# Three pairs of projection units computed with seven block products instead of eight

## The chip, the cores and the metric

The kernel runs on one NeuronCore of a Trainium2 chip. The metric is the device time of one execution in microseconds. The engines are TensorE (PE; its weight loads are shown apart as PEld), VectorE (DVE), ScalarE (ACT), GpSimd (POOL) and SyncE (SP), whose queue issues most of the DMAs.

## The reference, cut to what matters

One layer of an encoder over 1024 tokens of width 1024, in float32:

```python
h = rms_norm(x, g_norm1) * (1.0 + sc1) + sh1          # sc1, sh1, gt1, ...: rows of silu(c) @ w_ada + b_ada
proj = h @ w_in
qa, ka, va, qb, kb, vb, gates = split(proj)
qa, ka = rms_norm(qa, g_qa), rms_norm(ka, g_ka)       # per head of 64
o_a = neighbourhood_attention(qa, ka, va, rpb)        # 8 heads, 8 x 16 window on a 16 x 64 grid
qb, kb = rotary(rms_norm(qb, g_qb)), rotary(rms_norm(kb, g_kb))
o_b = merge of three dilated_window_attention         # 4 heads each, weighted by their softmax sums
merged = gate_a * (o_a @ w_proj_a) + gate_b * (o_b @ w_proj_b)      # gates: sigmoid(gates + b_gate)
x = x + gt1 * (merged @ w_o)
h2 = rms_norm(x, g_norm2) * (1.0 + sc2) + sh2
a, up = split(h2 @ w_ffn_in)
x = x + gt2 * ((silu(a) * up) @ w_ffn_out)
```

The change concerns `h @ w_in` for the columns of q, k and v.

## The kernel before, in words

Every float32 product is made of three passes: an operand is split into a high half (ScalarE copies it to the matmul's format) and a low half (VectorE or GpSimd subtracts), and the passes are high x high, high x low and low x high (`PASS`). `wsplit` does this for a block of weights (tiles `whi` and `wlo`, ten buffers each, lines 129 and 130); `hT` holds h transposed, split the same way, in two tiles.

The heads are grouped into ten *units* of two heads: units 0 to 5 are the dilated heads (kinds 0, 1, 2), units 6 to 9 the neighbourhood heads (kind 3). One unit's weights are 1024 x 384 (128 columns each of q, k and v). The loop over n runs the stage: step n = 8 u + t projects token tile t (128 tokens) of unit u. Its eight *chunks* (`proj_chunk`, one per 128 rows of the weights, three matmuls of 128x384 each, line 333) accumulate in one bank `ps_d`, of which there are two; `proj_post` then squares and normalizes q and k, rotates them for units 0 to 5 (GpSimd), and sends v to DRAM. Between the chunks stands the attention of units projected before: up to step 57 a *cluster* of items every second step (scores `ps_s`, softmax `P`, transposes `ps_t`, values `ps_v`), from step 58 (`PAIRED`) an item per step. The order on TensorE is the order of the code (manual schedule); on the other engines a scheduler sets it from priorities (`proj_post` stands above the rest), and SyncE's loads marked `pin` or `keep` keep the program's order.

Other work is spread over the same steps. `ada_step` adds up a row of the adaLN product on VectorE (line 322). `t_piece` makes, from h in DRAM (`h_d`), four *mixed* token blocks (sums and differences of quarters of h, split into halves, line 837 and after) and stores them in `t_d`; the gates use them for seven block products in place of eight (Strassen's scheme in Winograd's form). `gate_pre` runs the first gate products in steps 80 to 91 (line 783, chunks of 128x512). `combine_prep` and `combine_step` merge the dilated heads in steps 68 to 80. After step 91 come the remaining gate products, the merge, the output projection and the feed-forward part, which are also seven-product schemes where they are large.

## Time and profile before

| | us |
|---|---|
| median of 3 runs (lowest, highest) | 1488.75 (1488.46, 1489.19) |
| profiled execution, its own time | 1491.87 |
| its span | 1490.0 |
| TensorE busy | 1473.2 (99%) |
| TensorE weight loads busy | 1261.0 (85%) |
| VectorE busy | 1049.5 (70%) |
| ScalarE busy | 715.5 (48%) |
| GpSimd busy | 591.6 (40%) |

Matmuls are pipelined, so "busy" on TensorE means that something is in flight; what one costs is read from start to start. Windows of the trace are in us from the span's start. Step 10 begins at 78.1, step 28 at 182.7, step 58 at 365.4, step 76 at 486.1, step 80 at 514.5 and step 84 at 547.3: these are the starts of the first projection or gate matmul of the step on TensorE's timeline. VectorE's busy time is the time in which any of its instructions runs; neighbouring instructions overlap a little.

### The profile page before, as it was taken

What the parts mean: (1) busy time and instruction counts of PE and PEld (TensorE: products, weight loads), DVE (VectorE), ACT (ScalarE), POOL (GpSimd) and SP (SyncE); (2) the same over time, 40 slices, a digit from 0 to 9 for tenths busy, and PEclk for the clock granted to TensorE, in tenths of its full rate; (3) what the DMA queues carried; (4) which work ended last, traced back from release to release, by engine and by line L of the source; (5) the groups of instructions that cost most, each with busy time, mean ns of one, the idle gap of its engine ahead of it and who ended that gap; (6) DMA issues with size and microseconds to landing.
All of it is one profiled execution on the core that took longest, in us unless ns stands there. A gap on an engine that the chain in (4) does not pass through costs nothing. (4 is left out here: it accounts for less than half of the span.)

```text
span 1490.0 us, 24211 instructions
## 1 busy us (share of the span) xinstructions
PE 1473.2 (99%) x8168; PEld 1261.0 (85%) x8168; DVE 1049.5 (70%) x2042; ACT 715.5 (48%) x1855; POOL 591.6 (40%) x580
## 2 busy tenths in 40 slices
PE   8999999999999999999999999999999999999998
PEld 7999998999888877888888888888888888887886
DVE  6766766656768764476755596878777777598468
ACT  5566665566877755464422354323223333344442
POOL 0442332242100122356531402677777775104464
PEclk9999999999999999999999999999999999999999
DMA  9625554566143554774352325344533334898353
GB/s 362 248 85 166 170 166 130 180 218 199 65 154 115 183 199 156 283 270 133 119 190 88 111 85 183 121 149 159 177 107 108 109 109 145 285 373 275 98 156 99
DMA packets 156908, 250.54 MB, mean 168 GB/s; under 512 B 26832, under 2 KB 70512, under 8 KB 156016
## 3 DMA queue, kind: packets, MB, share of 16 engines
q1 hardware_dynamic: 138208, 235.35, 47.0%
q10 hardware_dynamic: 18576, 13.64, 2.8%
q8 instruction: 65, 1.06, 0.3%
q14 instruction: 59, 0.48, 0.1%
HBM read 184.06 MB, written 64.86 MB: 167 GB/s over the span
## 5 line engine op out<-in xcount | busy, mean ns | idle before, releaser
L333 PE MATMUL ps_d<-whi,hT 128*128 128x384 f32 x1152 | 312.1, 342 | 3.2 <-ACT whi L129 2.3
L129 ACT ACTIVATE whi<-raw 128x512 fp32r<-128x512 f32 (+2 forms) x313 | 182.7, 596 | 204.7 <-PE ps_s L1598 33.9
L130 POOL TENSOR_TENSOR wlo<-raw,whi 128x512 fp32r<-128x512 f32 (+2 forms) x122 | 159.1, 1311 | 280.3 <-ACT whi L129 236.5
L333 PEld LDWEIGHTS ps_d<-whi,hT 128*128 128x128 f32 x1152 | 210.9, 189 | 5.2 <-ACT whi L129 2.6
L130 DVE TENSOR_TENSOR wlo<-raw,whi 128x512 fp32r<-128x512 f32 (+1 forms) x191 | 170.8, 909 | 61.0 <-ACT whi L129 56.8
L333 PE MATMUL ps_d<-wlo,hT 128*128 128x384 f32 x576 | 194.0, 337 | 0.4 <-POOL wlo L130 0.4
L333 PEld LDWEIGHTS ps_d<-wlo,hT 128*128 128x128 f32 x576 | 109.2, 190 | 0.9 <-POOL wlo L130 0.8
L129 ACT ACTIVATE whi<-ws 128x512 fp32r<-128x512 f32 x60 | 37.7, 629 | 118.6 <-DVE ws L1445 72.0
L1378 POOL TENSOR_TENSOR e<-e,c 128x512 f32<-128x512 f32 x44 | 68.9, 1565 | 60.9 <-DVE c L1508 36.8
L783 PE MATMUL ps_d<-hT,whi 128*128 128x512 f32 x256 | 80.4, 395 | 0.0
L368 POOL TENSOR_TENSOR ra<-qn,rtab 128x64 f32<-128x64 f32 x48 | 16.9, 353 | 144.8 <-DVE qn L361 135.4
L130 POOL TENSOR_TENSOR wlo<-m,whi 128x512 fp32r<-128x512 f32 x35 | 51.5, 1480 | 54.3 <-ACT whi L129 54.3
L1376 ACT ACTIVATE e<-e 128x512 f32<-128x512 f32 x44 | 27.5, 631 | 92.1 <-DVE e L1511 65.8
L130 POOL TENSOR_TENSOR wlo<-gl,whi 128x512 fp32r<-128x512 f32 x26 | 36.3, 1412 | 71.6 <-ACT whi L129 70.0
L1428 PE MATMUL ps_v<-h2T,whi 128*128 128x512 f32 x192 | 59.2, 389 | 0.0
L1428 PE MATMUL ps_s<-h2T,whi 128*128 128x512 f32 x192 | 59.1, 389 | 0.0
L586 ACT ACTIVATE P<-P,st 128x256 f32<-128x256 f32 (+2 forms) x100 | 45.8, 460 | 26.9 <-DVE st L584 26.6
L1428 PE MATMUL ps_d<-h2T,whi 128*128 128x512 f32 x184 | 56.7, 390 | 0.0
L783 PEld LDWEIGHTS ps_d<-hT,whi 128*128 128x128 f32 x256 | 47.0, 188 | 9.3 <-issue 0.2
L1377 DVE TENSOR_TENSOR e<-e 128x512 f32<-128x512 f32 x44 | 42.5, 974 | 16.9 <-ACT e L1376 16.8
L354 DVE TENSOR_REDUCE ss<-sq 128x4 f32<-128x256 f32 x80 | 33.2, 415 | 26.3 <-ACT sq L351 25.9
L359 DVE SCALAR_TENSOR_TENSOR rz<-ss,ry 128x4 f32<-128x4 f32 x80 | 19.7, 246 | 45.1 <-ACT ry L358 44.8
(421 smaller groups left out, 4044.9 us busy)
## 6 DMA issues: line engine op xcount, KB each, us to landing
raw<-in_w_dram SPq DMA_DIRECT2D x139, 256.0 KB, 3.2
ga_d<-e SPq DMA_DIRECT2D x77, 256.0 KB, 2.0
raw<-ga_d SPq DMA_DIRECT2D x77, 256.0 KB, 2.7
wa<-in_wada_dram SPq DMA_DIRECT2D x32, 512.0 KB, 6.1
raw<-in_wqkv_dram SPq DMA_DIRECT2D x80, 192.0 KB, 4.7
m<-in_w_dram SPq DMA_DIRECT2D x44, 256.0 KB, 5.1
xt<-in_x_dram SPq DMA_DIRECT2D x16, 512.0 KB, 4.4
land<-in_wada_dram SPq DMA_DIRECT2D x16, 512.0 KB, 9.3
```

What stands on the lines that cost most here:

```text
L129: nc.scalar.activation(hi[:, :n], r, AF.Copy)
L130: (eng or nc.gpsimd).tensor_sub(lo[:, :n], r, fview(hi[:, :n]))
L333: nc.tensor.matmul(pd[:, :384], tok(a, k, t), U.w[k][b][:, :384], start=(k == 0 and i == 0), stop=(k == KT - 1 and i == 2))
L354: nc.vector.tensor_reduce(ss, sq.rearrange("p (h d) -> p h d", h=4), axis=mybir.AxisListType.X, op=ALU.add)
L359: nc.vector.scalar_tensor_tensor(z, ss, 64 * EPS, y2, op0=ALU.add, op1=ALU.mult)
L368: nc.gpsimd.tensor_tensor(v4(ra), v4(qn[:, :, 0:16]), tv(0, 0, 16), op=ALU.mult)
L586: nc.scalar.activation(C.P[h][:nq, c], C.P[h][:nq, c], AF.Exp, scale=-1.0, bias=nm, accum_out=sm)
L783: nc.tensor.matmul(pb, w[x][:, k * 128:(k + 1) * 128], b[y][:, k], start=(k == 0 and q == 0), stop=(k == 3 and q == 2))
L1376: nc.scalar.activation(sg, a, AF.Sigmoid)
L1377: nc.vector.tensor_mul(sg, sg, a)
L1378: nc.gpsimd.tensor_mul(sg, sg, up)
L1428: nc.tensor.matmul(pb, w[p][:, k * 128:(k + 1) * 128], b[q][:, k], start=(k == 0 and i == 0), stop=(k == 3 and i == 2))
```

## The change

Units 4 and 5, 6 and 7, 8 and 9 are projected as pairs. A pair is a product of 1024 tokens x 1024 by 1024 x 768, cut in two along all three sides, and `pair_units` computes it with seven products (`PROD`) instead of eight: each is 512 tokens (four tiles t) x 512 rows (four chunks k) x 384 columns. Three of the seven weight blocks are plain (p1, p2, w22); four are sums or differences that GpSimd makes (`mix`, tiles `chain`, which need a second load of four weight blocks). Four products take a mixed token block, streamed from `t_d` as tiles `smix` in the ring of weight buffers (two loads of 256 KB for each token tile). A bank now holds a partial sum, so `pair_evac` adds it on VectorE to two running sums A and B (in the quarter of `hT` that the pairs don't read), and `proj_post` first adds the last partial sum to q, k and v, on VectorE, where ScalarE copied them before.

The chunks of units 1 to 9 become one `stream`, and `quota` says how many a step takes: 8 in steps 8 and 9, 10 in steps 10 to 27, 7 from step 28; it ends in step 75. So a token tile is projected up to four and a half steps earlier, while the attention keeps its steps. `when` hangs loads, mixes and splits to places in the stream. Steps 76 to 83 take the first four gate phases, half a phase each. The mixed token blocks are made in steps 9 to 26 (16 to 47 before), `ada_step` runs twice in even steps of 28 to 57, `w1_combos` starts at 36 instead of 48. `hT` becomes eight quarters; `qn` has 9 buffers instead of 7, `stg` 2 instead of 3.

```diff
-GPREP = {77: (0, 0), 79: (0, 1), 82: (1, 0), ...
+GPREP = {74: (0, 0), 77: (0, 1), 82: (1, 0), ...
-W1MIX = 48
+W1MIX = 36
...
+        if acc is not None:
+            nc.vector.tensor_add(qn, acc[:, :256].rearrange("p (h d) -> p h d", h=4), pq)
+        vs = v_out(U, t, pd, acc)
...
-        nc.scalar.activation(sq, pd[:, :256], AF.Square)
-        nc.scalar.activation(qn, pq, AF.Copy, scale=-1.0 / 128)
+        nc.scalar.activation(sq, pd[:, :256] if acc is None else qn.rearrange("p h d -> p (h d)"), AF.Square)
+        if acc is None:
+            nc.scalar.activation(qn, pq, AF.Copy, scale=-1.0 / 128)
...
+        if acc is None:
             nc.scalar.activation(vs, pd[:, 256:384], AF.Copy)
+        else:
+            nc.vector.tensor_add(vs, acc[:, 256:384], pd[:, 256:384])
...
+    PROD = ("p1", "p2", "x1", "x2", "x4", "x3", "w22")
+    def pair_evac(nm, t, pd, ua, ub):
+        A, B, p = sums[0][:, t, :384], sums[1][:, t, :384], pd[:, :384]
+        if nm == "p2":
+            proj_post(unit_of(ua), t, pd, A)
+        elif nm == "x4":
+            proj_post(unit_of(ua), 4 + t, pd, B)
+        elif nm == "w22":
+            proj_post(unit_of(ub), t, pd, A)
+        else:
+            with tc.high_priority(PP):
+                if nm == "p1":
+                    nc.scalar.activation(A, p, AF.Copy)
+                elif nm == "x1":
+                    nc.vector.tensor_add(B, A, p)
+                elif nm == "x2":
+                    nc.vector.tensor_add(A, A, p)
+                    nc.vector.tensor_add(B, B, p)
+                else:
+                    nc.vector.tensor_add(A, A, p)
+            if nm == "x3":
+                proj_post(unit_of(ub), 4 + t, pd, B)
...
+                def mix(k=k, nm=nm, r=r):
+                    if nm == "x1":
+                        pin(nc.gpsimd.tensor_add(ch[k], ch[k], r[k]))
...
+                def split(k=k, nm=nm, r=r, w=w):
+                    w[k] = wsplit(ch[k] if nm in ("x1", "x2", "x3") else r[k], nc.vector if k % 2 else None)
+                when(s - 28 + 4 * k, load)
+                when(s - 12 + 2 * k, mix)
+                when(s - 7 + 2 * k, split)
+            for t in range(4):
...
+                if nm in TD:
+                    def sload(t=t, nm=nm, sm=sm):
+                        for q, tag in enumerate(("hi", "lo")):
+                            z = wp.tile([128, 512], F32R, tag=tag, bufs=NHL, name="smix")
+                            pin(nc.sync.dma_start(fview(z).rearrange("p (k q) -> p k q", k=4),
+                                                  t_d[q, TD[nm], :, :, 128 * t:128 * t + 128]))
+                    when(s + 4 * t - 10, sload)
...
+    for u in (1, 2, 3):
+        plain_unit(u)
+    for u in (4, 6, 8):
+        pair_units(u)
...
+    def quota(n):
+        return 8 if n < 10 else 10 if n < 28 else 7
...
+            if 76 <= n < 84:
+                chunks = gate_pre((n - 76) // 2)[4 * (n % 2):4 * (n % 2) + 4]
+            elif n >= 84:
+                chunks = gate_pre(n - 80)
...
-        if n >= 8 and (t != 7 or u > 8) and ada_state["i"] < 67:
-            ada_step()
-        if 2 <= u < 6 and t in (0, 2, 3, 4, 6, 7):
-            t_piece(2 * (u - 2) + t // 4, {0: 0, 2: 1, 3: 2}[t % 4])
+        for _ in range(0 if n < 8 else 2 if 28 <= n < PAIRED and n % 2 == 0 else 1):
+            if ada_state["i"] < 67:
+                ada_step()
+        for m in range(8):
+            if n - 9 - 2 * m in (0, 2, 3):
+                t_piece(m, max(n - 10 - 2 * m, 0))
```

TensorE around a cluster in the dilated stage, before (`hT_114` is the high half of h, `hT_408` the low half; lines 574 to 599 are a cluster's scores, values, q and k transposes and P transposes):

```order
L333 MATMUL ps_d<-whi,hT_114 128x384
L333 MATMUL ps_d<-wlo,hT_114 128x384
L333 MATMUL ps_d<-whi,hT_408 128x384
L574 MATMUL ps_s<-qk 128x256 x12
L619 MATMUL ps_v<-PT,v 64x128 x8
L408 MATMUL ps_v<-ident,qn 128x128 x4
L599 MATMUL ps_t<-ident,P 128x128 x8
L333 MATMUL ps_d<-whi,hT_114 128x384
L333 MATMUL ps_d<-wlo,hT_114 128x384
```

and after, in one of the four products with a mixed token block:

```order
L1151 MATMUL ps_d<-wlo,smix 128x384
L1151 MATMUL ps_d<-whi,smix 128x384
L597 MATMUL ps_s<-qk 128x256 x12
L642 MATMUL ps_v<-PT,v 64x128 x8
L428 MATMUL ps_v<-ident,qn 128x128 x4
L622 MATMUL ps_t<-ident,P 128x128 x8
L1151 MATMUL ps_d<-whi,smix 128x384
L1151 MATMUL ps_d<-wlo,smix 128x384
```

The cluster is the same; between two clusters stand 14 chunks instead of 16, and the stationary operand comes from the streamed tile.

VectorE at the end of a token tile, before (`ss` and `rz` are the sum of squares and the root's correction, `wlo` a low weight half, `tp` a mixed token block):

```order
L130 TENSOR_TENSOR wlo<-raw,whi 128x384
L843 TENSOR_TENSOR tp<-tp 128x512 x2
L354 TENSOR_REDUCE ss_3906<-sq 128x4
L359 SCALAR_TENSOR_TENSOR rz<-ss_3906,ry 128x4
L360 SCALAR_TENSOR_TENSOR rz<-rz,rv 128x4
L354 TENSOR_REDUCE ss_3971<-sq 128x4
L361 TENSOR_TENSOR qn<-qn,rz 128x256
```

and after, in a product (x3) that closes a running sum and ends a token tile (`hT` is here the running sum):

```order
L130 TENSOR_TENSOR wlo<-chain,whi 128x384
L1094 TENSOR_TENSOR hT<-hT,ps_d 128x384
L359 TENSOR_TENSOR qn<-hT,ps_d 128x256
L397 TENSOR_TENSOR vs<-hT,ps_d 128x128
L366 TENSOR_REDUCE ss_4154<-sq 128x4
L371 SCALAR_TENSOR_TENSOR rz<-ss_4154,ry 128x4
```

Three instructions that read the bank stand ahead of the reduction, and the next matmuls into that bank wait for them.

SyncE in the dilated stage, before (`wa` feeds `ada_step`, `rb` is a bias table):

```order
L120 DMA raw<-in_wqkv_dram 128x384
L297 DMA wa_5168<-in_wada_dram 128x1024
L455 DMA rb<-in_rbias_dram 128x768 x2
L120 DMA raw<-in_wqkv_dram 128x384 x2
L297 DMA wa_5380<-in_wada_dram 128x1024
```

and after:

```order
L120 DMA raw<-in_wqkv_dram 128x384
L1136 DMA smix<-t_d 128x4x128 x2
L120 DMA raw<-in_wqkv_dram 128x384
L305 DMA wa_5005<-in_wada_dram 128x1024
L1136 DMA smix<-t_d 128x4x128 x2
L120 DMA raw<-in_wqkv_dram 128x384
```

Between the raw weights stand the loads of the token tiles, two at a time.

## The prediction

> **What bounds the kernel now.** I read the page's busy table first, then the busy time by windows, then TensorE's timeline inside one projection step, then the waits, and last the instruction groups of VectorE in the stage that the change rewrites.

> ```profile
> span 1490.0 us, 24211 instructions
> PE 1473.2 (99%) x8168; PEld 1261.0 (85%) x8168; DVE 1049.5 (70%) x2042; ACT 715.5 (48%) x1855; POOL 591.6 (40%) x580
> ```

> TensorE has something in flight for 99% of the span, so a matmul that disappears is worth its time unless another engine cannot keep up. In the next view the first five rows are the stages of the loop over n: steps 10 to 27, 28 to 57, 58 to 75, 76 to 79 and 80 to 83. The last two rows are from the feed-forward part.

> ```profile
> core 0: us, PE busy (x) PEld busy (x) DVE busy (x) ACT busy (x) POOL busy (x), PEclk, DMA share, GB/s
> 78.10:182.70 104.60, 104.60 (x780) 98.11 (x779) 70.92 (x225) 67.03 (x247) 33.12 (x88) 1.00 0.40 128
> 182.70:365.40 182.70, 177.17 (x1301) 166.35 (x1300) 117.69 (x357) 112.05 (x400) 58.97 (x115) 0.98 0.55 176
> 365.40:486.10 120.70, 120.46 (x891) 107.89 (x889) 87.85 (x297) 89.06 (x301) 10.25 (x9) 1.00 0.40 126
> 486.10:514.50 28.40, 28.40 (x214) 25.58 (x212) 22.98 (x68) 21.07 (x68) 5.12 (x4) 1.00 0.51 157
> 514.50:547.30 32.80, 32.19 (x203) 24.67 (x202) 20.47 (x49) 17.90 (x49) 5.18 (x4) 1.00 0.66 229
> ...
> 840.00:880.00 40.00, 40.00 (x191) 33.38 (x190) 35.50 (x58) 21.91 (x46) 10.31 (x7) 1.00 0.35 109
> ...
> 1320.00:1360.00 40.00, 38.30 (x167) 30.71 (x166) 38.95 (x57) 14.17 (x23) 6.33 (x4) 1.00 0.99 359
> ```

> TensorE is the bound in all five stages, and VectorE has room: 64% busy in steps 28 to 57, 73% in steps 58 to 75. The last two rows show how far VectorE can be filled: at 89% TensorE lost nothing, at 97% it lost 1.7 of 40 us (the DMA engines were full there too, at 0.99).

> The price of one projection chunk (three passes over 128x384) is read from the start times, since the durations overlap:

> ```profile
> 152.66 0.33 PE L333 MATMUL ps_d<-wlo,hT 128*128 128x384 f32 x1
> ...
> 153.18 0.33 PE L333 MATMUL ps_d<-wlo,hT 128*128 128x384 f32 x1
> ...
> 153.62 0.98 PE L574 MATMUL ps_s<-qk 64*128 64x256 f32 x12
> 154.53 0.89 PE L619 MATMUL ps_v<-PT,v 128*64 128x64 f32 x16
> 155.35 0.66 PE L408 MATMUL ps_v<-ident,qn 128*128 128x128 f32 x4
> 155.84 1.04 PE L599 MATMUL ps_t<-ident,P 128*128 128x128 f32 x8
> 156.63 0.42 PE L333 MATMUL ps_d<-whi,hT 128*128 128x384 f32 x1
> ```

> One chunk is 153.18 - 152.66 = 0.52 us, and the attention work of a pair of steps is 156.63 - 153.62 = 3.0 us. A chunk of the gate products is three matmuls of 128x512; six of them take 1.36 us elsewhere, so it costs 0.68.

> ```profile
> 1358.03 1.36 PE ps_s L1598 x6
> ```

> **The change, part by part.**

> *TensorE.* A pair of units costs 7 x 4 x 4 = 112 chunks in place of 128, so three pairs drop 48 chunks: 48 x 0.52 = 25.0 us. By stage: steps 10 to 27 take ten chunks instead of eight, +36 chunks, +18.7 us. Steps 28 to 75 take seven (the last one three), -52 chunks: -15.6 us in steps 28 to 57 and -11.4 in 58 to 75. Steps 76 to 79 lose 32 chunks and gain 16 gate chunks, -16.6 + 10.9 = -5.8 us (rounded), and steps 80 to 83 lose those 16, -10.9. The sum is -25.0, if the other engines follow.

> *VectorE, steps 28 to 57.* These are the prices, first from that window, then from steps 58 to 75:

> ```profile
> L322 DVE SCALAR_TENSOR_TENSOR acc<-wa,cact,acc 128x512 f32<-128x512 f32 x23 | 18.5, 802 | 4.5 <-DMA wa<-in_wada_dram 4.4
> L130 DVE TENSOR_TENSOR wlo<-raw,whi 128x384 fp32r<-128x384 f32 x12 | 10.5, 874 | 3.2 <-ACT whi L129 3.1
> L359 DVE SCALAR_TENSOR_TENSOR rz<-ss,ry 128x4 f32<-128x4 f32 x30 | 8.6, 285 | 23.0 <-ACT ry L358 22.9
> L433 DVE TENSOR_TENSOR qk<-ps_v,qk 128x256 fp32r<-128x256 f32 x16 | 7.4, 465 | 0.0
> L843 DVE TENSOR_TENSOR tp<-tp 128x512 fp32r<-128x512 f32 x10 | 6.5, 682 | 1.7 <-ACT tp L840 1.7
> L837 DVE TENSOR_TENSOR tp<-tp 128x512 f32<-128x512 f32 x5 | 3.4, 686 | 3.9 <-DMA tp<-h_d 3.9
> L839 DVE TENSOR_TENSOR tp<-tp 128x256 f32<-128x256 f32 x5 | 2.1, 428 | 0.0
> L838 DVE TENSOR_TENSOR tp<-tp 128x256 f32<-128x256 f32 x5 | 2.1, 419 | 0.0
> L320 DVE TENSOR_SCALAR acc<-wa,cact 128x512 f32<-128x512 f32 x3 | 1.5, 487 | 0.0
> L286 DVE TENSOR_TENSOR brow<-ps_t,brow 128x128 f32<-128x128 f32 x3 | 0.9, 297 | 1.3 <-PE ps_t L283 1.3
> ```

> ```profile
> L322 DVE SCALAR_TENSOR_TENSOR acc<-wa,cact,acc 128x512 f32<-128x512 f32 x14 | 11.2, 802 | 3.6 <-DMA wa<-in_wada_dram 3.5
> L359 DVE SCALAR_TENSOR_TENSOR rz<-ss,ry 128x4 f32<-128x4 f32 x18 | 2.9, 159 | 6.9 <-ACT ry L358 6.9
> L717 DVE TENSOR_TENSOR oacc<-oacc,ps_t 128x512 f32<-128x512 f32 x4 | 2.7, 683 | 0.0
> ```

> ```profile
> L130 DVE TENSOR_TENSOR wlo<-raw,whi x12: 544/959/1249, 201.0 to 355.7; 128x384 fp32r<-128x384 f32 x12
> ```

> The first fence holds groups with their mean (ns) after the comma, the last row the shortest, median and longest low half. The counts come from the two programs' code. Added: 29 adds of the accumulator to q and k (256 wide, out of PSUM, 0.465 like line 433), 13.5 us; 29 of v (128 wide, 0.297), 8.6; 32 partial sums 384 wide (between 0.465 and the 0.683 of 512 wide, so 0.57), 18.2; 14 more low weight halves at 0.874, 12.2; 16 more steps of the adaLN row with two opening ones and three biases (0.802, 0.487, 0.297), 14.7. Removed: the mixed token blocks, which are now made before step 28, 6.5 + 3.4 + 2.1 + 2.1 = 14.1. Net 53.1 us of durations. The 20 rows of this window add up to 133 us while the engine was busy 117.7, because neighbours overlap, so 0.88 of it counts: 47, and VectorE needs about 164 us. TensorE's plan for the stage is 182.7 - 15.6 = 167.1, of which some 9 were idle or at half clock before (next fence). So VectorE goes from 64% to 98% of the plan. [...]

> *VectorE, steps 58 to 75.* Added 19 x (0.465 + 0.297) + 16 x 0.57 + 8 x 0.874 = 30.6; removed adaLN rows, 11.2, 2 x 0.487 and 2 x 0.297; net 17.8 x 0.88 = 16, so 104 us against a plan of 120.7 - 11.4 = 109.3, or 95%. Steps 70 to 73 hold the posts of units 8 and 9 and the merging of the dilated heads at once.

> *ScalarE* gains the high weight halves and loses the copies of q, k and v out of PSUM. With about the work of before in a shorter stage it would be busy 89 of 109 us in steps 58 to 75, 82%, and less elsewhere, so I cost it at nothing: the chunks of TensorE hide it. If they did not, its late copies would show as waits of VectorE. The prologue and all that follows step 92 are unchanged.

> *DMA, steps 28 to 57.* 0.55 of 182.7 us moved 176 GB/s x 182.7 us = 32.2 MB, or 3.1 us of all engines per MB. The mixed token blocks add 64 loads of 256 KB (16.8 MB), the weights 6.1, adaLN 4.2, and 7.8 of mixed-block traffic leave: +19.3 MB, +60 us, 161 in all. This is 96% of the plan. SyncE issues these loads in program order; a load that waits for a free weight buffer holds up the ones behind it, among them the raw weights of the next product.

> *Waits.* In the code a low half is asked for seven chunks before its first use (k = 0) down to four (k = 3), that is 2 to 4 us and the attention work between them, where before six of the eight halves of a unit were asked for about a step (5.7 us) ahead. What such a wait costs, the trace shows once, at the first step of unit 5:

> ```profile
> 256.32 0.19 PEld L333 LDWEIGHTS ps_d<-whi,hT 128*128 128x128 f32 x1
> 259.14 0.29 PEld L333 LDWEIGHTS ps_d<-whi,hT 128*128 128x128 f32 x1 [2.63 <-ACT whi L129]
> 260.23 0.29 PEld L333 LDWEIGHTS ps_d<-wlo,hT 128*128 128x128 f32 x1 [0.79 <-POOL wlo L130]
> 260.39 0.66 PEld L333 LDWEIGHTS ps_d<-whi,hT 128*128 128x128 f32 x2
> 261.04 0.33 PEld L333 LDWEIGHTS ps_d<-wlo,hT 128*128 128x128 f32 x1
> ...
> 262.00 0.33 PEld L333 LDWEIGHTS ps_d<-wlo,hT 128*128 128x128 f32 x1
> ```

> 3.4 us idle, and then chunks at 0.97 (261.04 to 262.00) instead of 0.52 for about 6.8 us, which loses 3.4 more: 6 to 7 us for one event. [...]

> **The sum.** Steps 10 to 27: VectorE gets the 14 us of mixed blocks and four token tiles more, at most 21 us: 92 of 123.3, so TensorE's +18.7 stands. Steps 28 to 57: VectorE and DMA both need 161 to 164; at a reachable 95% that is 173 us, -9.7 against 182.7 rather than -15.6. Steps 58 to 75: 104 / 0.95 = 110, and four for the crowd at 70 to 73, 114: -6.7. Steps 76 to 83: -5.8 - 10.9. Together -14.4. The profiled execution was 1491.87 us, 3.1 over the median of the runs; on the median this is 1488.75 - 14.4 = 1474.4, and I give 1475.

> **The rivals.**

> *All of it.* VectorE and DMA follow: -25.0, and if the 9 us of stalls in steps 28 to 57 also go, -34: 1455 to 1464. For it: at 89% of VectorE no loss. Against: 98% and 96% at once.

> *DMA is the bound.* If loads land late often enough that steps 28 to 57 take what they took before, the sum is -14.4 + 9.7 = -5, and a few stalls more make it no change: about 1486. For it: the share of 0.96; against: these loads are asked for ten chunks ahead.

> *Late weight halves, slower.* The halves on a full VectorE come after TensorE needs them. There are 21 products, each with four; one event costs 6 to 7 us, so three take the whole forecast back, and five give 1475 + 32 = 1507. For it: the one event of before came in exactly this form. Against: short waits, under 2 us, did not lower the clock in the row of 1320 to 1360 us.

> [...]

> **How the numbers follow.** Chances: part of the gain as summed 0.42, all of it 0.20, no change 0.10, late halves 0.18, mutual blocking 0.10. A measurement here can tell about 0.2% (3 us) from no change. Faster is 0.62, the same 0.10, slower 0.28. The range runs from half of the way into the full gain, 1459, to four late events after the partial gain, 1500; if it is faster, I expect 1459 to 1484.

> **What would show it.** Right: the window of steps 10 to 27 grows by 19 us, steps 80 to 83 shrink by 11, VectorE is busy over 90% and the DMA share near 0.9 in steps 28 to 57, and that stage takes 168 to 178 us. Wrong: waits of TensorE for low halves or for landed token blocks of more than 15 us in all, or a granted clock under 0.95 there (late halves); line 371, the successor of 359, over 400 ns (blocking); VectorE below 85% with TensorE gapless (all of it).

## The result and the profile after

The changed kernel took 1533.55 us (median of 4 runs, 1532.01 to 1534.09) where the kernel before took 1488.97 in the same session: ratio 1.029, 95% interval 1.0268 to 1.0313. It is 44.6 us slower; the forecast was 1475, its range ended at 1500. The profiled span is 1532.3 us against 1490.0, so 42.3 us have to be found.

From the page, the span and the busy table:

```profile
span 1532.3 us, 24444 instructions
PE 1470.1 (96%) x8024; PEld 1246.5 (81%) x8024; DVE 1118.4 (73%) x2210; ACT 715.4 (47%) x1807; POOL 668.0 (44%) x640
```

TensorE has 144 matmuls fewer (48 chunks of three, as planned), and its share fell from 99% to 96%. Nobody took its place as the busiest engine: VectorE stands at 73%. That is the first hint that the loss is waiting, not work. The same five stages as before, in the same columns (steps 10 to 27, 28 to 57, 58 to 75, 76 to 79, 80 to 83):

```profile
core 0: us, PE busy (x) PEld busy (x) DVE busy (x) ACT busy (x) POOL busy (x), PEclk, DMA share, GB/s
77.60:203.10 125.50, 123.56 (x888) 116.63 (x886) 98.01 (x274) 81.72 (x284) 54.46 (x105) 1.00 0.61 195
203.10:413.30 210.20, 178.31 (x1235) 161.16 (x1235) 151.37 (x439) 105.14 (x353) 95.89 (x134) 0.89 0.75 235
413.30:533.00 119.70, 111.00 (x810) 97.05 (x807) 103.47 (x349) 89.45 (x289) 34.37 (x33) 0.99 0.65 193
533.00:562.10 29.10, 24.14 (x168) 18.11 (x166) 18.35 (x57) 16.57 (x48) 0.56 (x1) 0.99 0.53 163
562.10:587.50 25.40, 22.37 (x147) 16.27 (x146) 18.06 (x46) 12.64 (x36) 2.56 (x3) 0.95 0.63 199
```

| steps | before | after | change | predicted |
|---|---|---|---|---|
| 10-27 | 104.6 | 125.5 | +20.9 | +18.7 |
| 28-57 | 182.7 | 210.2 | +27.5 | -9.7 |
| 58-75 | 120.7 | 119.7 | -1.0 | -6.7 |
| 76-83 | 61.2 | 54.5 | -6.7 | -16.7 |
| the rest | | | +1.6 | 0 |

Most of the miss, 37 of 57 us, is in steps 28 to 57. The row of that stage tells its form: TensorE idle 210.2 - 178.3 = 31.9 us, and a granted clock of 0.89. The granted clock was 0.50 for 44.4 us in five stretches (the last section has them), and TensorE was busy for 31.2 us of these, which is up to another 16 us lost. Without both the stage would have taken about 163 us; VectorE is 72% busy and the DMA engines 0.75, so neither was full.

What TensorE waited for there, from the table of waits (total, times, longest):

```profile
PE ps_d L1151 <- DVE vs L397: 9.7, 4, 4.6
PE ps_d L1151 <- DMA smix<-t_d: 8.2, 2, 6.9
PE ps_d L1151 <- ACT whi L129: 6.1, 3, 4.8
PE ps_d L1151 <- POOL wlo L130: 3.6, 3, 1.7
PE ps_d L1151 <- ACT qn L364: 1.9, 1, 1.9
PE ps_d L1151 <- ACT hT L1087: 1.7, 1, 1.7
PE ps_d L1151 <- DVE wlo L130: 1.7, 1, 1.7
```

There are three kinds. A bank of PSUM is not yet read (lines 397 and 1087: 11.4 us; the 1.9 us of line 364 end where the stage begins and belong to step 27), a weight half is not ready (lines 129 and 130: 11.4 us), a mixed token block has not landed (8.2 us). On TensorE's timeline the long ones stand in five places (of the first, three waits; of the others the longest):

```profile
228.05 0.44 PE L1151 MATMUL ps_d<-wlo,smix 128*128 128x384 f32 x1 [1.65 <-DVE wlo L130]
...
229.74 0.45 PE L1151 MATMUL ps_d<-whi,smix 128*128 128x384 f32 x1 [1.07 <-ACT whi L129]
230.93 0.69 PE L1151 MATMUL ps_d<-wlo,smix 128*128 128x384 f32 x1 [0.74 <-POOL wlo L130]
...
277.38 0.69 PE L1151 MATMUL ps_d<-whi,smix 128*128 128x384 f32 x1 [4.82 <-ACT whi L129]
...
309.97 0.66 PE L1151 MATMUL ps_d<-whi,smix 128*128 128x384 f32 x1 [6.93 <-DMA smix<-t_d]
310.43 0.52 PE L1151 MATMUL ps_d<-wlo,smix 128*128 128x384 f32 x1
...
311.49 0.52 PE L1151 MATMUL ps_d<-wlo,smix 128*128 128x384 f32 x1
...
345.40 0.66 PE L1151 MATMUL ps_d<-whi,hT 128*128 128x384 f32 x1 [4.62 <-DVE vs L397]
...
391.29 0.66 PE L1151 MATMUL ps_d<-whi,hT 128*128 128x384 f32 x1 [3.15 <-DVE vs L397]
```

These are steps 32, 39, 42, 47 and 54. Behind the wait of step 42 a chunk takes 311.49 - 310.43 = 1.06 us instead of 0.52, at a granted clock of 0.50: the half clock of the forecast. Between the places the plan holds: 34 of the 66 steps from 10 to 75 are longer or shorter than before by their chunks times 0.52 us, to within 0.15 us.

Two queues show how a wait comes about. GpSimd, ahead of the second place:

```profile
250.72 1.00 POOL L130 TENSOR_TENSOR wlo<-raw,whi 128x384 fp32r<-128x384 f32 x1
265.78 0.32 POOL L384 TENSOR_TENSOR ra<-qn,rtab 128x64 f32<-128x64 f32 x1 [14.06 <-DVE qn L377]
...
267.42 2.44 POOL L1122 TENSOR_TENSOR chain<-raw,chain 128x384 f32<-128x384 f32 x2
```

GpSimd stood idle for 14.06 us, since the next instruction in its order was the rotary embedding of a token tile that VectorE had not finished. The weight sums of product x3 (line 1122) stood behind it, and the high halves behind them. The second queue is SyncE's own; its waits in the 15 us ahead of the third place (290 to 305 us), and its last issues there:

```profile
SPq L1136 <- PE ps_d L1151: 5.5, 1, 5.5
SPq L889 <- POOL w1m L885: 4.8, 1, 4.8
SPq L889 <- POOL w1m L887: 1.6, 1, 1.6
```

```profile
297.25 2.85 SPq L889 DMA_DIRECT2D w_d<-w1m  x3
300.53 1.79 SPq L877 DMA_DIRECT2D w1m<-in_w_dram  x4
...
304.54 1.32 SPq L1136 DMA_DIRECT2D smix<-t_d  x2
```

One mixed block waited 5.5 us for a ring buffer; the stores of GpSimd's feed-forward sums (line 889) then waited 4.8 + 1.6 us for the sums, and the four loads for the next sums followed them. The mixed block of step 42 was issued at 304.54, when TensorE had already run out, and landed 5 us later.

### The profile page after: what moved, and what is told of

It is laid out like the page before. It is cut to its first block, busy times and chain, and to the rows that moved or that the text cites. A ratio compares the mean times of both kernels' runs of the same rounds, so it can differ in the third digit from the quotient of the medians.

```text
span 1532.3 us, 24444 instructions
## 1 busy us (share of the span) xinstructions
PE 1470.1 (96%) x8024; PEld 1246.5 (81%) x8024; DVE 1118.4 (73%) x2210; ACT 715.4 (47%) x1807; POOL 668.0 (44%) x640
## 3 DMA queue, kind: packets, MB, share of 16 engines
q8 instruction: 64, 1.05, 0.3%
## 5 line engine op out<-in xcount | busy, mean ns | idle before, releaser
L129 ACT ACTIVATE whi<-raw 128x512 fp32r<-128x512 f32 (+2 forms) x313 | 182.6, 594 | 224.1 <-PE ps_t L1762 33.9
L130 POOL TENSOR_TENSOR wlo<-raw,whi 128x512 fp32r<-128x512 f32 (+2 forms) x116 | 153.1, 1327 | 207.0 <-ACT whi L129 151.2
L130 DVE TENSOR_TENSOR wlo<-raw,whi 128x512 fp32r<-128x512 f32 (+1 forms) x197 | 174.7, 900 | 61.5 <-ACT whi L129 57.3
L1151 PE MATMUL ps_d<-whi,smix 128*128 128x384 f32 x384 | 112.5, 359 | 15.0 <-DMA smix<-t_d 8.2
L341 PE MATMUL ps_d<-whi,hT 128*128 128x384 f32 x384 | 101.0, 338 | 0.0
L1151 PE MATMUL ps_d<-whi,hT 128*128 128x384 f32 x288 | 84.0, 354 | 16.4 <-DVE vs L397 9.7
L129 ACT ACTIVATE whi<-ws 128x512 fp32r<-128x512 f32 x60 | 37.7, 628 | 119.4 <-DVE ws L1609 83.5
L1151 PEld LDWEIGHTS ps_d<-whi,smix 128*128 128x128 f32 x384 | 74.3, 199 | 18.1 <-issue 7.6
L130 POOL TENSOR_TENSOR wlo<-m,whi 128x512 fp32r<-128x512 f32 x35 | 51.9, 1492 | 55.5 <-ACT whi L129 55.5
L1151 PE MATMUL ps_d<-wlo,smix 128*128 128x384 f32 x192 | 67.7, 353 | 5.3 <-POOL wlo L130 3.6
L384 POOL TENSOR_TENSOR ra<-qn,rtab 128x64 f32<-128x64 f32 x48 | 22.0, 459 | 115.2 <-DVE qn L375 64.9
L130 POOL TENSOR_TENSOR wlo<-gl,whi 128x512 fp32r<-128x512 f32 x26 | 35.9, 1394 | 82.4 <-ACT whi L129 82.4
L1151 PEld LDWEIGHTS ps_d<-whi,hT 128*128 128x128 f32 x288 | 54.4, 194 | 20.1 <-issue 12.2
L341 PEld LDWEIGHTS ps_d<-whi,hT 128*128 128x128 f32 x384 | 69.6, 188 | 0.5 <-issue 0.4
L341 PE MATMUL ps_d<-wlo,hT 128*128 128x384 f32 x192 | 64.2, 334 | 0.0
```

The lines of the kernel that those rows point to most:

```text
L129: nc.scalar.activation(hi[:, :n], r, AF.Copy)
L130: (eng or nc.gpsimd).tensor_sub(lo[:, :n], r, fview(hi[:, :n]))
L341: nc.tensor.matmul(pd[:, :384], tok(a, k, t), U.w[k][b][:, :384], start=(k == 0 and i == 0), stop=(k == KT - 1 and i == 2))
L384: nc.gpsimd.tensor_tensor(v4(ra), v4(qn[:, :, 0:16]), tv(0, 0, 16), op=ALU.mult)
L1151: nc.tensor.matmul(pd[:, :384], lhs, w[k][b][:, :384], start=(k == 0 and i == 0), stop=(k == 3 and i == 2))
```

## The experiments

Each ratio is to runs of the kernel before on the same chip (medians 1490.6 to 1492.0). "After" is the changed kernel. The kernel before moved by 3 us between sessions (1489.0 to 1492.0), so differences of that size between runs of different sessions mean nothing.

**The feed-forward sums back at their place.**

```diff
-W1MIX = 36
+W1MIX = 48
```

> Only the feed-forward weight sums of GpSimd go back from steps 36-44 to steps 48-56, as in the kernel before; nothing is left out. Theory W (these sums and their 256 KB loads crowd out the projection's own in steps 36-46): the stalls near 268, 303 and 336 us shrink, steps 28-57 fall from 210 to about 190 us and the time to about 1514. Theories Q (queue of loads), H (late weight halves) and A (VectorE's adds): the crowd only moves, 1528-1538.

1521.43 us, ratio 1.0205 (1.0186 to 1.0224), 12 us less than after. Steps 28 to 57 fell to 194.8; steps 42, 43 and 47 lost their stalls, steps 32 and 39 kept theirs.

```profile
203.20:398.00 194.80, 173.98 (x1235) 157.06 (x1235) 149.46 (x442) 104.64 (x353) 93.14 (x133) 0.93 0.79 247
```

So theory W is part of it: two of the five places. Step 55, where the sums now are, got a new one (10.5 us instead of 6.7).

**No streamed mixed blocks.** Mixed products read resident tokens.

```diff
-                if nm in TD:
+                if False:
...
-                        if nm in TD:
-                            lhs = sm[a][:, 128 * k:128 * k + 128]
-                        else:
-                            lhs = tok(a, k + (0 if nm == "p1" else 4), t + (4 if nm == "x4" else 0))
+                        lhs = tok(a, k + (0 if nm == "p1" else 4), t + (4 if nm == "x4" else 0))
```

> The products with mixed tokens take their stationary operand from the resident token blocks, so the 96 loads of streamed mixed blocks are left out (the values of units 4-9 are not those of the reference); all matmuls, sums and weight halves stay. Theory Q (SyncE waits in its queue for a ring buffer that these loads need, and the DMA engines fill up in bursts): the 32 us of SyncE's waits for that ring go, weights land in time, steps 28-57 fall to 180 us or less and the time to about 1503. Theory H or A: only the one 6.9 us wait for a landed block and its half clock go, 1518-1526.

1517.58 us, ratio 1.0182 (1.0153 to 1.0211), 16 us less than after: at the edge of what theories H and A expected (1518), and 15 us above theory Q's 1503.

```profile
202.60:400.70 198.10, 172.14 (x1234) 155.99 (x1234) 156.30 (x443) 105.83 (x357) 98.68 (x135) 0.93 0.55 169
```

With the DMA share down to 0.55 the stage still took 198 us; steps 32 and 39 were as long as in after, steps 42 and 47 lost their stalls, and step 46 got one (4.7 us for line 397). The DMA engines were not the bound, and the streamed loads are one cause among several.

**No adds of partial products.**

```diff
-            proj_post(unit_of(ua), t, pd, A)
+            proj_post(unit_of(ua), t, pd)
...
-                elif nm == "x1":
-                    nc.vector.tensor_add(B, A, p)
...
```

> The adds of partial products on VectorE are left out, and q, k, v are copied out of PSUM by ScalarE as before (units 4-9 then hold the last product alone). Theory A (a bank of PSUM is emptied too late because VectorE has a burst of adds at the end of each product, every four chunks): the waits for line 397 near 336, 345 and 391 us go with their half clock, about 20 us: 1513. Theory Q or H: the time stays at 1526-1534.

1528.13 us, ratio 1.0248 (1.0231 to 1.0265): 5 us less. The two stalls at line 397 did go, as theory A says (step 47: 15.5 to 7.1 us, step 54: 9.3 to 5.2), but steps 46, 51 and 59 grew by 12 us together, with waits for ScalarE's copies (lines 1087 and 364) and for a landed block. ScalarE copies q, k and v here where VectorE added, so the run prices an exchange, not VectorE alone.

**No sums of weights.**

```diff
...
-                        pin(nc.gpsimd.tensor_add(ch[k], ch[k], r[k]))
...
-                    w[k] = wsplit(ch[k] if nm in ("x1", "x2", "x3") else r[k], nc.vector if k % 2 else None)
+                    w[k] = wsplit(r[k], nc.vector if k % 2 else None)
```

> The sums of weights on GpSimd and the extra loads of their 12 buffers are left out; the halves are split straight from the loaded weights (units 4-9 then hold other values). Theory H (load, sum on GpSimd, high half on ScalarE, low half on VectorE or GpSimd stand one behind the other, and the last of them is late): the waits for lines 129 and 130 near 228 and 268-282 us go with their half clock, about 25 us: 1508. Theory Q or A: 1522-1534.

1519.67 us, ratio 1.0183 (1.0161 to 1.0205), 14 us less, where theory H expected 25. In steps 28 to 57 the gain is 21 us, the largest of the four; steps 32 and 39 lost their stalls, step 42 kept its own (7.3 us for a landed block). Theory H holds for those two places.

**The rest of the change, without block products.**

```diff
-    for u in (1, 2, 3):
-        plain_unit(u)
-    for u in (4, 6, 8):
-        pair_units(u)
+    for u in range(1, 10):
+        plain_unit(u)
...
-        return units[u], (j + 4) % 8 if u in (5, 7, 9) else j
+        return units[u], j
...
-        return 8 if n < 10 else 10 if n < 28 else 7
+        return 8 if n < 10 else 10 if n < 28 else 8
```

> Units 4-9 stay plain (eight products, as many chunks as before), with the rest of the change kept: ten chunks in steps 10-27 and eight from step 28, four and a half steps of lead, mixed blocks made early, two adaLN steps in even steps, feed-forward sums at steps 36-44, gate products from step 76. If the loss sits in the products (theories H, Q, A): the stalls of after are absent and the time is that of before or up to 9 us less, 1480-1490. If it sits in the run-ahead or in what was moved with it (W among it): 1500 or more.

1496.8 us, ratio 1.0037 (1.0022 to 1.0052): slower than before, by 5 us, with the same number of chunks, and between the two expectations. Its windows (steps 10 to 27, 28 to 57, 58 to 75, 76 to 83):

```profile
78.20:201.50 123.30, 123.30 (x886) 116.69 (x885) 97.61 (x272) 79.20 (x277) 52.98 (x102) 1.00 0.63 199
201.50:378.20 176.70, 175.16 (x1325) 164.22 (x1324) 117.44 (x364) 106.30 (x401) 51.60 (x97) 1.00 0.51 160
378.20:497.00 118.80, 117.94 (x865) 105.62 (x861) 75.95 (x260) 84.84 (x294) 14.15 (x12) 1.00 0.27 80
497.00:550.60 53.60, 46.48 (x311) 34.20 (x310) 35.65 (x101) 30.43 (x87) 2.90 (x3) 0.97 0.58 187
```

The stalls of steps 28 to 57 are gone; the stage is even 6 us shorter than before. The last row is the finding. Steps 10 to 27 paid 123.3 - 104.6 = 18.7 us for the chunks made ahead, exactly as priced, and steps 76 to 83 give back 61.2 - 53.6 = 7.6 instead of 16.7. There TensorE is idle 7.1 of 53.6 us, in waits that belong to the gate (lines 806 and 837), to the merge of the dilated heads (lines 720, 729 and 740) and to the neighbourhood attention, which is what runs after step 58 (lines 556 and 562):

```profile
509.41 0.73 PE L806 MATMUL ps_d<-hT,whi 128*128 128x512 f32 x2 [0.91 <-ACT ga L837]
...
524.46 0.63 PE L729 MATMUL ps_t<-ident,fb 128*128 128x128 f32 x4 [2.17 <-DVE fb L720]
532.32 0.55 PE L556 MATMUL ps_t<-ident,P 128*128 128x128 f32 x3 [1.49 <-ACT PT L562]
539.50 0.52 PE L556 MATMUL ps_t<-ident,P 128*128 128x128 f32 x3 [1.15 <-DVE oacc L740]
```

**All four edits together, and three of them.** The edits of the first four runs; then the same with the adds kept.

> The four edits of the runs before together: feed-forward sums back at steps 48-56; streamed mixed blocks, sums of weights and adds of partial products left out (units 4-9 then hold other values); all 528 chunks stay. If Q, H, A and W are all there is, TensorE runs steps 28-57 at its plan, 160-165 us, and the 48 chunks come in full: 1458-1468. If something else takes the time: 1480 or more.

> As the run with all four, but the adds of partial products stay on VectorE (streamed blocks and sums of weights left out, feed-forward sums at steps 48-56). Theory A: the adds cost what they cost with everything else gone, 10-20 us over that run. If VectorE's adds only matter when the weights are late already: within 4 us of it.

1496.44 us, ratio 1.0024 (1.0007 to 1.0042), and 1501.61, ratio 1.0058 (1.0042 to 1.0074). The adds cost 5 us with all else gone, as alone. But the four edits, 47 us one by one, gave 37 together and left the kernel 28 to 38 us above the expectation: of this, by the stages, 10 us in steps 76 to 83 (54.4 us, as in the plain run), 3 in steps 10 to 27, about 15 in steps 28 to 57 (173.7 instead of 159), 6 in steps 58 to 75. The longest waits left in steps 28 to 57 were for banks of PSUM, 3.9 us at step 54: TensorE's last tile there was done at 355.5 us, and ScalarE copied q and k out of the bank (line 364) only at 358.91, behind the softmax of a cluster, which had waited 1.75 us for VectorE.

**Loads, sums and halves earlier.**

```diff
-W1MIX = 36
+W1MIX = 48
...
-                when(s - 28 + 4 * k, load)
-                when(s - 12 + 2 * k, mix)
-                when(s - 7 + 2 * k, split)
+                when(s - 30 + 4 * k, load)
+                when(s - 18 + 2 * k, mix)
+                when(s - 9 + 2 * k, split)
```

> Nothing is left out. Feed-forward sums back at steps 48-56, and in the pairs the raw weights are loaded two chunks earlier, summed on GpSimd six chunks earlier (ahead of the rotary embedding of the token tiles that end in between) and split two chunks earlier. Theory H: the stalls at steps 32 and 38-39, 19 us, go: 1502 against 1521 for the feed-forward sums alone. Theory Q: the earlier loads and halves hold ring buffers longer, SyncE waits more, and the time stays at 1515-1525.

1513.28 us, ratio 1.015 (1.0124 to 1.0176), 8 us less than with the feed-forward sums alone. The stalls of steps 32 and 38-39 went, as theory H says, but less than half of their 19 us came back: step 43, without a stall in the run with the feed-forward sums alone, now waited 4.86 us for line 397, and step 51 1.9 us for a landed block.

**An extra bank, and the feed-forward sums later.**

```diff
...
-                        sm["pd"] = bank("d")
+                        tiles[0] += 1
+                        sm["pd"] = bank("s" if step[0] < PAIRED and step[0] % 2 == 0 and tiles[0] % 2 else "d")
...
```

> Nothing is left out. As the run with early loads, sums and halves (1513), and in even steps before step 58, where no attention runs, every other tile of four chunks goes to a bank of the scores instead of one of the projection's two. Theory B (a tile now lasts 2.1 us instead of 4.2, and two banks are not emptied that fast): the waits of TensorE for lines 364, 397 and 1087 to 1094, 14 us in that run, go with their half clock, and steps 28-57 fall from 194 to 175-180 us: 1495-1500. If the readers of the bank are late for another reason, a third bank only delays the wait: 1508-1515.

> As the run with the extra bank, with the feed-forward sums at steps 60-68, where GpSimd is 30% busy. Theory W: the two waits for landed mixed blocks near steps 51-55 (about 5 us and a half clock) go: 1488-1492 if the bank works, 1502-1508 if it does not. Against: the dilated steps from 58 on have work in every step, and the waits may move there.

1512.48 us, ratio 1.0135 (1.0103 to 1.0167), the same as without the bank; and 1521.58, ratio 1.0191 (1.0163 to 1.0219), 9 us more. A third bank in the even steps brought nothing: at step 43 the scores, which need the borrowed bank back, now waited 5.13 us for line 397 to read it. More banks in the odd steps were not tried. Sums at steps 60 to 68 shortened steps 28 to 57 to 179.6 us and made steps 58 to 75 132.1.

**One part on the kernel before: mixed blocks early.**

```diff
-        if 2 <= u < 6 and t in (0, 2, 3, 4, 6, 7):
-            t_piece(2 * (u - 2) + t // 4, {0: 0, 2: 1, 3: 2}[t % 4])
+        for m in range(8):
+            if n - 9 - 2 * m in (0, 2, 3):
+                t_piece(m, max(n - 10 - 2 * m, 0))
```

> The kernel before with one part of the change alone: the mixed token blocks are made in steps 9-26 instead of 16-47. No run-ahead, no block products. The 5.6 us that TensorE lost at steps 40 and 41 stood behind a store of a mixed block that waited on SyncE; if that is so, they go, with the 1.3 us of steps 47 and 53 at most: 1481-1484. That is also the measure for what the run-ahead costs: the plain run (1497) less this one. If the stall comes from ScalarE's order instead, it stays: 1488-1492.

1486.69 us, ratio 0.9965 (0.9949 to 0.998): faster than the kernel before, by about 4 us, and between the two expectations. Its windows for the same four stretches as in the plain run:

```profile
78.20:185.40 107.20, 105.20 (x780) 98.00 (x778) 85.41 (x252) 71.87 (x252) 38.94 (x91) 1.00 0.63 207
185.40:360.00 174.60, 173.79 (x1302) 163.94 (x1302) 104.29 (x330) 106.49 (x393) 57.20 (x114) 1.00 0.42 134
360.00:480.70 120.70, 120.46 (x889) 107.87 (x888) 87.92 (x297) 88.79 (x301) 10.26 (x9) 1.00 0.40 125
480.70:541.70 61.00, 60.49 (x415) 50.38 (x414) 44.01 (x120) 39.52 (x117) 10.86 (x9) 1.00 0.60 200
```

Steps 28 to 57 became 8.1 us shorter, steps 40 and 41 alone 6.1, and steps 10 to 27 took 2.6 us more for the blocks. Steps 76 to 83 are as long as before, 61.0 us with TensorE busy 60.5. The 10 us between this run and the plain one are therefore what the run-ahead and what goes with it cost.

**v out of its ring of two buffers; feed-forward sums before the first pair.**

```diff
...
-        vs = v_out(U, t, pd, acc)
+        v_out(U, t, pd, acc, vs)
...
-        A, B, p = sums[0][:, t, :384], sums[1][:, t, :384], pd[:, :384]
+        A, B, p = sums[0][:, t, :384], sums[1][:, t, :384], pd[:, :384]
+        va, vb = sums[0][:, t, 384:], sums[1][:, t, 384:]
...
```

> The changed kernel with one edit, nothing left out: v of a token tile of a pair is not put into the ring of two 128x128 buffers but into the free last 128 columns of the partial sums' rows, so that no add waits until the store of v two tiles earlier has landed. Theory V (two buffers suffice when a tile takes 8 chunks, 4.2 us, and not when it takes 4, 2.1 us, since a store lands 3.4-3.8 us after its issue): TensorE's four waits for line 397, 9.7 us, go with the half clock behind them, 15-20 us: 1513-1519. Theory A (VectorE is late with its work): at most 3 us less, 1530-1534.

> Nothing is left out: feed-forward sums at steps 48-56, earlier loads, sums and halves (together 1513), and v in the sums' free columns. Theory V: the waits of TensorE for lines 397, 364 and 1087, 14 us in that run, and a half clock of about 7 us go: 1493-1500. Theory A: 1508-1514.

> As the run with earlier halves and v in the free columns, with the feed-forward sums at steps 16-24, ahead of the first pair, where GpSimd has no sums of weights. Theory W: the waits for landed mixed blocks near steps 51-55, some 8 us with half clock, go and none comes in their place: 1486-1492. Theory Q alone (the loads are late whatever else SyncE does): within 3 us of that run.

1532.86 us, ratio 1.0286 (1.0264 to 1.0308); 1511.09, ratio 1.014 (1.0122 to 1.0158); 1506.79, ratio 1.0106 (1.0091 to 1.0121). Theory V fell: the ring is not the cause, alone (1 us) or with early halves (2 us). The trace of after agrees: there VectorE's instructions of line 397 waited only 0.3 us for stores of v in steps 28 to 57. Feed-forward sums ahead of the pairs took off 4 us more and cost some in steps 10 to 27 (128.1). In the last of the three, TensorE waited 5.89 us at step 44:

```profile
308.60 0.69 PE L1153 MATMUL ps_d<-whi,hT 128*128 128x384 f32 x1 [5.89 <-ACT hT L1089]
```

and ScalarE's timeline shows where the copy that frees the bank (line 1089) stood:

```profile
304.44 0.49 ACT L610 ACTIVATE P<-P,st 128x256 f32<-128x256 f32 x1
...
307.67 0.51 ACT L129 ACTIVATE whi<-chain 128x384 fp32r<-128x384 f32 x1
308.08 0.47 ACT L1089 ACTIVATE hT<-ps_d 128x384 f32<-128x384 f32 x1
```

TensorE had completed its last tile at 302.7 us; the copy ran at 308.08, behind the softmax of a whole cluster and a high half. ScalarE was busy 104 of 183 us in that stage: not full, but in order.

**One adaLN step per step.**

```diff
...
-        for _ in range(0 if n < 8 else 2 if 28 <= n < PAIRED and n % 2 == 0 else 1):
-            if ada_state["i"] < 67:
-                ada_step()
+        if n >= 8 and (t != 7 or u > 8) and ada_state["i"] < 67:
+            ada_step()
```

> The changed kernel with one edit, nothing left out: one step of the adaLN row per step of the loop and none in every eighth, as before, instead of two in even steps from step 28 on. Theory R (the 16 extra steps, 0.79 us each on VectorE and 256 KB of loads each, stand ahead of the adds and halves that TensorE waits for): some of the five stalls shrink, steps 28-57 fall by 10 us or more, and steps 58-75 lengthen by less than 4: 1520-1526. If it is cover that VectorE has anyway (72% busy): 1530-1536.

> As the run with earlier halves, v in the free columns and the feed-forward sums at steps 16-24 (1507), with one adaLN step per step. Theory R: the 5.9 us wait at step 44, where an adaLN step stands between the reads of scores on VectorE, goes: 1494-1500. Otherwise 1504-1509.

1532.59 us, ratio 1.0278 (1.0256 to 1.03), and 1516.77, ratio 1.0178 (1.0163 to 1.0194): no gain alone, and 10 us more than the run it builds on. The time that theory R gave did not come. In the profiled run of the first (1526.36, the fastest of its four), steps 28 to 57 did fall, to 195.5, and steps 58 to 75 rose to 127.5: the work only moved.

**The mixed blocks a little later, on the kernel before.**

```diff
-        if 2 <= u < 6 and t in (0, 2, 3, 4, 6, 7):
-            t_piece(2 * (u - 2) + t // 4, {0: 0, 2: 1, 3: 2}[t % 4])
+        for m in range(8):
+            if n - 10 - 3 * m in (0, 1, 2):
+                t_piece(m, n - 10 - 3 * m)
```

> The kernel before with the mixed token blocks made a little later than in the run with that part alone (1487): one block's load, differences and low part in three successive steps from step 10 to 33. If the 1.5 us that step 19 and the 1.1 us that steps 10-27 otherwise lost there came from two blocks at once, they go and steps 40-41 stay as short: 1484-1485. If not: 1486-1488.

1487.44 us, ratio 0.9984 (0.9973 to 0.9995): no better than two blocks at once. Steps 10 to 27 took as long (107.3), and steps 31 to 33 lost 2.1 us. The run with the blocks in steps 9 to 26 keeps the lowest median of the study, by less than the noise.

## Why the prediction was wrong, step by step

*TensorE's price: right.* 0.52 us per chunk holds in after wherever nothing waits, and steps 10 to 27 of the plain run took +18.7 us to the tenth. After has 2.2 more there, a wait of 1.9 us for line 364 at step 27.

*VectorE's load: nearly right.* 151 us in steps 28 to 57 where 164 were summed, 103.5 in steps 58 to 75 where 104 were. The prices of the new rows, from the groups of instructions of steps 28 to 57:

```profile
L359 DVE TENSOR_TENSOR qn<-hT,ps_d 128x256 f32<-128x256 f32 x29 | 12.0, 412 | 4.2 <-PE ps_d L1151 4.2
L397 DVE TENSOR_TENSOR vs<-hT,ps_d 128x128 f32<-128x128 f32 x28 | 7.8, 279 | 0.3 <-DMA v_d<-vs 0.3
L371 DVE SCALAR_TENSOR_TENSOR rz<-ss,ry 128x4 f32<-128x4 f32 x27 | 6.1, 225 | 8.8 <-ACT ry L370 8.7
L1089 DVE TENSOR_TENSOR hT<-hT,ps_d 128x384 f32<-128x384 f32 x8 | 4.4, 548 | 2.7 <-PE ps_d L1151 2.7
```

0.412, 0.279 and 0.548 us against 0.465, 0.297 and 0.57. The DMA load was right too: 0.75 x 210.2 = 158 us against 161.

*"At a reachable 95% that is 173 us": the step that failed.* It turned a load into a time, as if the stage were limited by how much an engine can do. The stage took 210 us with VectorE at 72% and DMA at 0.75. What limits it is when an operand comes, and the forecast priced that at nothing in the likeliest case. The argument for the cover, loads "asked for ten chunks ahead", failed at the queue: 6.93 us for a block that SyncE issued late, behind stores that waited for GpSimd. The term should have held five events of 6 to 12 us: steps 32, 38 with 39, 42, 47 and 54 were together 41 us longer than in the plain run, less its eighth chunk.

*Late weight halves: the right rival, given too little and drawn too narrowly.* It had the price of an event, the half clock, and "five give 1507". Its signs came: 19.6 us of waits for halves and landed blocks, where 15 was the sign, and a clock of 0.89, where 0.95 was. Five places it was, but two of them were late halves; one was a landed block and two were unread banks, and the waits reached 6.9 us, so that an event cost 8 us in the mean and not 6 to 7. Its counter-argument, that waits under 2 us do not lower the clock, did not hold at step 32, where waits of 1.65 and 1.07 us stood ahead of a granted clock of 0.50 (230.17 to 237.00 us). Steps 58 to 83 came on top.

*ScalarE "at nothing": wrong.* In steps 28 to 57 its busy time fell to 105 us (112 before), and TensorE still waited 6.1 us for its high halves (line 129) and 1.7 for a copy out of PSUM (line 1087), after 1.9 at the end of step 27 (line 364). The forecast had looked for late copies among the waits of VectorE.

*Steps 58 to 75, -6.7: right in kind, short in size.* -1.0. TensorE was idle for 119.7 - 111.0 = 8.7 us, in the plain run for 0.9. Of the 8.7, 4.7 are waits of the merge's transposes (line 729) in steps 72 to 75, about what the forecast gave the crowd at steps 70 to 73; the rest it had at nothing.

*Steps 76 to 83, -16.7: wrong, and not for the products' sake.* -6.7 in after and -7.6 in the plain run, which has none. The projection chunks taken out there had covered the serial work of the neighbourhood attention, of the merge and of the gate; once they are gone, that work sets the step: 7.1 us of idle TensorE in the plain run, of the 9.1 us that the stage fell short there. This step was costed by TensorE's chunks alone, though the forecast's own rule was to name the cover of what is moved. The run-ahead pays its 18.7 us in a stage where TensorE is the bound and gets less than half back.

*VectorE and GpSimd blocking each other: not shown.* Line 371 took 225 ns, less than the 285 of line 359 before, where over 400 was the sign. Single low halves took up to 1637 ns (1249 before), but their mean on raw weights was 859 ns (874 before), and the load did not grow. That VectorE waits out instructions of GpSimd was the author's estimate, and no run shows it.

*The range's lower end.* 1459 lies in the middle of the full gain, 1455 to 1464, and not half of the way from 1475 to it, which is about 1467. It changes nothing here.

*What stays open.* Feed-forward sums (12 us), streamed blocks (16), sums of weights (14) and adds (5) are each shown to cost time, and they overlap. Why steps 28 to 57 still lost some 15 us with all four out of the way is shown only in part: one wait of that run, 3.9 us at step 54, and one of 5.9 us in the run with the sums before the first pair are read from ScalarE's timeline, where the copy stands behind a softmax. No run changed the order of ScalarE or VectorE alone. The extra bank in even steps, the ring of v and the adaLN steps were tried and brought nothing.

## What to carry to other kernels

When TensorE is nearly gapless, an exchange of its work for loads, sums and halves has to be judged by the longest chain from load to operand and by the queue in which each link stands, not by the busy share of the engines: here none beside TensorE was above 75% in the stage that lost 27 us. Work moved ahead only pays if the place it leaves has something else for TensorE; look there for a serial chain that the moved work had covered. And try the parts of a change one by one: the part that pays (mixed blocks made earlier, 4 us) was hidden in a change that cost 45.

## What was not expected of the hardware

```profile
226.76:230.17 3.41, 1.05 (x3) 0.48 (x3) 3.41 (x8) 1.70 (x6) 2.70 (x5) 1.00 0.79 159
230.17:237.00 6.83, 6.09 (x20) 6.08 (x20) 4.74 (x11) 0.95 (x4) 4.03 (x10) 0.50 1.02 304
```

Waits of 1.65 and 1.07 us left TensorE busy for 1.05 of the 3.41 us; ahead of the other four it was busy for 0.95 to 1.38 us. The run with v in the free columns shows that one wait of 2.40 us (342.06 to 344.45) was enough as well:

```profile
341.97:345.38 3.41, 1.01 (x8) 0.71 (x9) 1.93 (x8) 1.13 (x4) 0.99 (x1) 1.00 0.28 57
345.38:348.79 3.41, 3.41 (x30) 2.96 (x29) 3.41 (x9) 1.86 (x8) 0.00 (x0) 0.50 1.08 272
```

There the first matmuls behind the wait took 0.41, 0.33 and 0.34 us (344.45, 344.70 and 344.88), where the first behind the wait of step 42 took 0.66, and the clock fell 0.9 us after the wait, so what this wait cost can't be read from the matmul right behind it.
